# An encoder kernel: Lambda's exponential moved to the first down projection, no preparing transfers beside the output projection, another rounding order in the first two seven-product tiles

## The chip, the cores and the metric

The kernel runs on one core of a Trainium2 chip. A core has a matrix engine (TensorE, PE in the profile; its weight loads are shown as PEld), a vector engine (VectorE, DVE), a scalar engine (ScalarE, ACT), a general engine (GpSimd, POOL) and a sync engine (SyncE, SP), each with its own queue of instructions that it works off in order. SP, ACT and POOL can start transfers between device memory and on-chip memory. The metric is the device time of one execution in microseconds, taken as the median of several runs.

## The reference

A hybrid encoder of two layers on 512 positions of width 1024, float32:

```python
for l in range(DEPTH):
    h = rms_norm(x, norm_g[l, 0])
    x = x + 0.5 * swiglu(h, ffn_w_gate[l, 0], ffn_w_up[l, 0], ffn_w_down[l, 0])
    h = rms_norm(x, norm_g[l, 1])
    proj = h @ w_in[l]
...
    lam = jnp.exp(jnp.sum(lq[0] * lq[1])) - jnp.exp(jnp.sum(lq[2] * lq[3])) + lam_init
    yb = diff_attention(..., lam, lam_init, diff_subln_g[l], ...)
...
    x = x + merged @ w_o[l]
    h = rms_norm(x, norm_g[l, 2])
    x = x + 0.5 * swiglu(h, ffn_w_gate[l, 1], ffn_w_up[l, 1], ffn_w_down[l, 1])
return rms_norm(x, final_g)
```

`swiglu(h, g, u, d)` is `(silu(h @ g) * (h @ u)) @ d` with an inner width of 2816. Between the two halves of a layer stands the mixer: three attention branches (neighbourhood, differential, windowed with grouped keys), each gated, added up as `merged`, and projected by `w_o`. Lambda is one number per layer, an exponential of a sum minus another, used by the differential branch only.

## The kernel before

**Products.** Every float32 matrix product is made from operands split in two: a high part rounded by ACT (`scalar.copy` into the type fp32r) and a low part, the rest, made by DVE (`tensor_tensor` subtract). high x high, high x low and low x high are added up in PSUM. `weights` (L85) loads a weight tile of 512 KB through SP into one of three buffers `raw` and splits it (L92 on ACT, L93 on DVE); `parted` (L97) splits what is on the chip already (L100, L101).

**Order.** The program goes through ffn(0,0), mixer 0, ffn(0,1), ffn(1,0), mixer 1, ffn(1,1), the numbers being layer and half. A scheduler sorts the instructions of each engine by readiness and their place in the program. `tc.issue_after(x)` puts what is written in its block behind `x`, on the engine of `x` alone; `Seven.in_order` (L513) holds all instructions of its block in the written order on every engine.

**The seven-product tiles.** Each half has 22 tiles of 128 inner columns for gate and up. The first two (in ffn(0,0) four) are made as plain products and go through `gated` (L385): scale by the norm, Silu on ACT (L389), multiply (L390), split (ACT L124, DVE L126). The others go through `Seven.tile` (L593), which makes a tile's gate and up, each for two halves of the positions and of the channels, in seven block products where eight would be plain. Their moving sides are sums of blocks of the normed input, made once per half by `Sides` (L393, starting with L404 on DVE). Their weights are `wa` (the gate tile itself), `w31` and `w24` (two sums of weight blocks) and `w22`. A tile does, in this order: product 1 with `wa`; the copy of the former tile's bank (`sum22`, L688); the split of the next tile's `wa` (`next_wa`) and of its own `w24`; the former tile's Silu (L693); the copy of its own bank (L641); product 5 with `w31` (bank `pr`); product 4 of the former tile with `w22`; product 6 with `w24` (bank `mm`, moving side `pair`), which writes on into the bank that L641 has to read first; then products 2, 3 (bank `pv` and `pr`) and 7. Its scratch `gu` has two buffers, so the first such tile takes over the buffer of the first `gated`. In the first tile of a half, `next_wa` comes later (L661).

**Prepared sums.** In ffn(0,0) `w31` and `w24` are summed on the spot, by an accumulating transfer and by `others` on DVE (L551). For the three other halves they are prepared in device memory ahead of time by `prepare` (L447): each step copies a weight tile twice (ACT's queue, L474 and L475) and adds blocks onto copies of earlier tiles (three transfers on POOL's queue, L465). 27 steps make one half. `ahead_by` (L486) issues steps at a pace: each call of `weights` adds `owed[1]`, each seven-product tile adds `PACE["seven"]`, and a step is issued whenever a whole one is owed. `PACE` (L34) holds the rates by stage: a mixer calls `weights` 66 times before the output projection and 8 times in it; a down projection calls it 24 times. `drained` (L495) issues at the start of a half whatever of its steps is left.

**Small values.** `small_values` (L252) computes Lambda of both layers and some scaled constants, inside tile 8 of ffn(0,0), in written order, together with the first part of `position_tables` (L211); the rest of the position tables follows in tile 9. Silu and Exp need different tables on ACT; the change of table shows in the trace as ACT_TABLE_LOAD.

**Output projection.** The last loop of `mixer` (L1375) multiplies by `w_o` in eight tiles, adds to the residual (L1380, in tiles `lg` of the mixer's memory), stores the residual by POOL's queue (`x_keep`, L68) and makes the next norm's parts.

Of the kernel before, what the change touches and what calls it, by code (L numbers as in the profile page):

```python
# [11 lines left out]
F32 = mybir.dt.float32  # L12
# [4 lines left out]
P = 128  # L17
# [13 lines left out]
T5_STEPS = (8, 12, 16, 23, 32, 46, 64, 91)  # L31
GBUFS = 2 * MF
NO_WAIT = mybir.DependencyInfo(mybir.DependencyClass.NoSync, mybir.DependencyReason.DATA)
PACE = {"mixer": (0.42, 0.3), "seven": {(0, 1): 0.25}, "down": {(0, 0): 0.3, (0, 1): 0.4, (1, 0): 0.25}}  # L34
LOW_FIRST = (2, 4, 7)
WIDE, WIDE_FIRST = frozenset((2, 3, 4, 5, 6, 7)), frozenset((3, 4, 5))

# [2 lines left out]
def encoder(ctx: ExitStack, tc: tile.TileContext, a: dict, out: bass.AP):  # L40
# [13 lines left out]
    def f(ap):  # L54
        return ap.bitcast(F32)
# [23 lines left out]
    nc.scalar.activation(early, nhalf, AF.Silu)  # L79


    loaded, lower = [], []
    prepared, ahead, due, owed, queue = {}, [], [], [0.0, 0.0], {}

    def weights(src, width=1024):  # L85
# [163 lines left out]
            )  # L249
            own.append([bg, sg, sink, lq])  # L250

    def small_values(fp):  # L252
        for l in range(DEPTH):
            bg, sg, sink, lq = own[l]
            lam_init = 0.8 - 0.6 * math.exp(-0.3 * l)
            nc.vector.tensor_scalar_mul(bg, bg, 0.5)
            nc.vector.tensor_scalar_mul(sg, sg, 1.0 - lam_init)
            nsink = small.tile([P, 8], F32, tag=f"nsink{l}", name="nsink", bufs=1)
            nc.vector.tensor_scalar_mul(nsink, sink, -1.0)
            lp = fp.tile([P, 2, 64], F32, tag="g", name="lp", bufs=GBUFS)  # L260
            nc.vector.tensor_tensor(out=lp, in0=lq[:, :, 0, :], in1=lq[:, :, 1, :], op=ALU.mult)
            ls = small.tile([P, 2], F32, tag="ls", name="ls", bufs=1)
            nc.vector.reduce_sum(ls, lp, axis=mybir.AxisListType.X)
            nc.scalar.activation(ls, ls, AF.Exp)
            nlam = small.tile([P, 1], F32, tag=f"nlam{l}", name="nlam", bufs=1)
            nc.vector.tensor_tensor(out=nlam, in0=ls[:, 1:2], in1=ls[:, 0:1], op=ALU.subtract)
            nc.vector.tensor_scalar_add(nlam, nlam, -lam_init)
            own[l] = bg, sg, sink, nsink, nlam
# [12 lines left out]
    def ffn(l, i, h, nxt=None):  # L281

        with tc.tile_pool(name="ffn", bufs=1) as fp, ExitStack() as order:
# [11 lines left out]
            start, plain = (2, 4) if first else (0, 2)  # L295
            for m in range(start, MF):
                if m >= plain:
                    if first and m == plain + 4:
                        tables = position_tables(fp)
                        with tiles.in_order():  # L300
                            next(tables)
                            small_values(fp)
                    if first and m == plain + 5:
                        with tiles.in_order():
                            list(tables)
                    if m == plain:
# [52 lines left out]
            for m in range(KC):  # L359
                parts = []  # L360
                for c in range(0, MF, 8):
                    n = min(8, MF - c)
                    parts.append((c, n, cols(weights(a["w_down"][l, i, m, :, c * P : (c + n) * P]), n)))
                ps = mm_tile()
                for c, n, w in parts:
                    if m == 0 and c == 8:
                        tiles.flush()
                    for k in range(n):
                        nc.tensor.matmul(ps, w[k][0], ghi[c + k], start=c + k == 0, stop=False)  # L369
                        nc.tensor.matmul(ps, w[k][0], glo[c + k], start=False, stop=False)  # L370
                    for k in range(n):
                        nc.tensor.matmul(ps, w[k][1], ghi[c + k], start=False, stop=c + k == MF - 1)  # L372
                advance(m, ps, h.rb, fp, nxt)

    def quarters(fp):

        return fp.tile([P, 5, H], F32, tag="gu", name="gu", bufs=2)

    def keep(fp, un, ghi, glo):

        hi, lo = split(un, fp, "g", GBUFS)
        ghi.append(hi)
        glo.append(lo)

    def gated(h, fp, pg, pu, ghi, glo):  # L385
        t = quarters(fp).rearrange("p a c -> p (a c)")
        gn, un = t[:, 0:S], t[:, S : 2 * S]
        nc.vector.tensor_tensor(out=gn, in0=pg, in1=h.rb, op=ALU.mult)
        nc.scalar.activation(gn, gn, AF.Silu)  # L389
        nc.vector.tensor_tensor(out=un, in0=pu, in1=gn, op=ALU.mult)  # L390
        keep(fp, un, ghi, glo)

    class Sides:  # L393

# [107 lines left out]
    class Seven:  # L502


        def __init__(self, l, i, h, fp, sides, ghi, glo):
            self.at, self.h, self.fp, self.sides, self.out = (l, i), h, fp, sides, (ghi, glo)
            self.ready = (l, i) in prepared
            self.wide = WIDE if self.ready else WIDE_FIRST
            self.raw, self.even, self.sums, self.a22, self.wa, self.w31 = {}, {}, {}, {}, {}, {}
            self.tail, self.behind = (), {}  # L510

        @contextmanager
        def in_order(self):  # L513
# [79 lines left out]
        def tile(self, m):  # L593

            h, fp, sides, last = self.h, self.fp, self.sides, m == MF - 1
            first = not sides[0].t[3:]
            tail = iter(self.tail)

            def rest():
# [29 lines left out]
            with self.in_order():  # L629
# [1 line left out]
                self.fetch(m + 2)  # L631
                self.product(1, one, blocks(wa), [s.b11 for s in sides], start=True)
                rest()
                if not first:
                    next_wa()
                elif not self.ready:
                    self.others(m)
                parted(self.even.pop(m), w24)
                rest()
                u1 = self.halves(1)  # L640
                nc.scalar.copy(g[:, 0:u1], one[:, 0:u1])  # L641
# [60 lines left out]
                    add(q[3], one[:, 0], q[3])  # L702
                nc.vector.scalar_tensor_tensor(out=un, in0=un, scalar=-1.0, in1=gn, op0=ALU.mult, op1=ALU.mult)

            def kept():
                nc.scalar.copy(hi, un)
                nc.vector.tensor_tensor(out=lo, in0=un, in1=f(hi), op=ALU.subtract)

            self.tail = sum22, gate, fourth, up, kept

    def opening(l, i, h, fp, ghi, glo):

# [165 lines left out]
    def mixer(l, h, nxt):  # L878
        with tc.tile_pool(name="mix", bufs=1) as mp:
# [491 lines left out]
            while later:  # L1371
                step(None)
                run([last.pop(0)] if last else [])
            run([merge(2, m) for m in range(4)])
            for m in range(KC):  # L1375
                w = weights(a["w_o"][l, m])
                ps = mm_tile()
                product(ps, cols(w, KC), mh, ml)
                t = x_tile(m, l_tile())
                nc.vector.scalar_tensor_tensor(out=t, in0=ps, scalar=0.5, in1=t, op0=ALU.mult, op1=ALU.add)  # L1380
                x_keep(m, t, nxt.step)
                nxt.chunk(m, t, lambda: mp.tile([P, S], F32, tag="sq", name="sq", bufs=2))
# [8 lines left out]
    for l in range(DEPTH):  # L1391
# [2 lines left out]
        n2 = Norm(3 * l + 2, gain(l, 2))  # L1394
        owed[1] = PACE["mixer"][l]
        mixer(l, n1, n2)
        owed[1] = 0
        if l + 1 < DEPTH:
            h = Norm(3 * l + 3, gain(l + 1, 0))
            ffn(l, 1, n2, h)  # L1400
# [90 lines left out]
```

## Time and profile before

| | us |
|---|---|
| median of 3 runs | 2423.55 |
| lowest, highest | 2421.86, 2423.68 |
| the profiled execution | 2423.72 |
| its span, first to last instruction | 2421.9 |
| PE busy | 2393.2 (99%) |
| DVE busy | 1709.7 (71%) |
| ACT busy | 1330.8 (55%) |
| POOL busy | 361.1 (15%) |

Matmuls are pipelined and their ends are modelled, so a busy PE isn't PE at its peak. A row of the timeline holds the start, the length, the engine, the line of the kernel, the operation, what it writes and reads by the program's names, its shapes and the count of instructions merged into the row; a bracket at its end holds the idle time of the engine before it and what ended it. "issue" stands for time in which the engine waited for nothing that the profile shows. PEq, SPq and the like are the engines' queues.

### The profile page before, as it was taken

What the parts mean: (1) busy time and instruction counts of PE and PEld (TensorE: products, weight loads), DVE (VectorE), ACT (ScalarE), POOL (GpSimd) and SP (SyncE); (2) the same over time, 40 slices, a digit from 0 to 9 for tenths busy, and PEclk for the clock granted to TensorE, in tenths of its full rate; (3) what the DMA queues carried; (4) which work ended last, traced back from release to release, by engine and by line L of the source; (5) the groups of instructions that cost most, each with busy time, mean ns of one, the idle gap of its engine ahead of it and who ended that gap; (6) DMA issues with size and microseconds to landing.
All of it is one profiled execution on the core that took longest, in us unless ns stands there. A gap on an engine that the chain in (4) does not pass through costs nothing.

```text
span 2421.9 us, 34919 instructions
## 1 busy us (share of the span) xinstructions
PE 2393.2 (99%) x12762; PEld 2049.1 (85%) x12762; DVE 1709.7 (71%) x3061; ACT 1330.8 (55%) x2433; POOL 361.1 (15%) x524
## 2 busy tenths in 40 slices
PE   9999999999999999999999999999999999999998
PEld 7899888888888878888888888888888888888887
DVE  7999335766666669995389983467666666899832
ACT  6566225756566446663256652367565674566632
POOL 3100014432101120001200001144121100000000
PEclk9999999999999999999999999999999999999999
DMA  6576689986557697868745556788655624455532
GB/s 200 160 188 172 201 252 264 239 208 158 138 154 202 195 235 229 253 222 246 201 161 188 187 192 201 222 224 200 183 159 162 158 93 139 155 191 186 172 120 70
DMA packets 149771, 452.86 MB, mean 187 GB/s; under 512 B 18264, under 2 KB 23688, under 8 KB 148640
## 3 DMA queue, kind: packets, MB, share of 16 engines
q1 hardware_dynamic: 89856, 278.50, 34.8%
q0 software_dynamic: 40352, 107.36, 22.1%
q10 hardware_dynamic: 19392, 64.78, 7.5%
q8 instruction: 100, 1.64, 0.3%
q14 instruction: 71, 0.58, 0.1%
HBM read 428.52 MB, written 138.44 MB: 234 GB/s over the span
## 4 chain that ended last, share of the span: by engine, by line
PE 90%; DVE 4%; issue 2%; ACT 1%; DMA 1%; POOL 1%; SPq 0%; POOLq 0%; ACTq 0%; DVEq 0%
PE mm L562 17%; PE pr L562 8%; PE mm L117 8%; PE mm L115 8%; PE mm L114 8%; PE mm L369 5%; PE mm L372 5%; PE mm L370 5%; PE pv L562 4%; PE mm L1277 2%; PE av L1059 2%; PE mm L1273 2%; PE mm L1272 2%; PE t L1049 1%; PE s L1004 1%
## 5 line engine op out<-in xcount | busy, mean ns | idle before, releaser
L92 ACT CAST whi<-raw 128x1024 fp32r<-128x1024 f32 (+1 forms) x258 | 265.4, 1032 | 403.5 <-PE mm L370 185.4
L93 DVE TENSOR_TENSOR wlo<-raw,whi 128x1024 fp32r<-128x1024 f32 (+1 forms) x258 | 310.4, 1203 | 233.3 <-ACT whi L92 118.6
L114 PE MATMUL mm<-h,whi 128*128 128x512 f32 x800 | 318.2, 398 | 0.0
L115 PE MATMUL mm<-h,whi 128*128 128x512 f32 x800 | 314.1, 393 | 0.0
L369 PE MATMUL mm<-g,whi 128*128 128x512 f32 x528 | 205.4, 389 | 0.0
L370 PE MATMUL mm<-g,whi 128*128 128x512 f32 x528 | 205.4, 389 | 0.0
L117 PE MATMUL mm<-h,wlo 128*128 128x512 f32 x800 | 197.9, 389 | 0.0
L101 DVE TENSOR_TENSOR wlo<-raw,whi 128x1024 fp32r<-128x1024 f32 x156 | 184.2, 1218 | 5.5 <-ACT whi L100 5.5
L117 PEld LDWEIGHTS mm<-h,wlo 128*128 128x128 f32 x800 | 150.0, 188 | 31.3
L115 PEld LDWEIGHTS mm<-h,whi 128*128 128x128 f32 x800 | 150.5, 188 | 29.1 <-DVE h L146 0.3
L114 PEld LDWEIGHTS mm<-h,whi 128*128 128x128 f32 x800 | 150.4, 188 | 28.8 <-ACT h L145 0.3
L100 ACT CAST whi<-raw 128x1024 fp32r<-128x1024 f32 x156 | 156.9, 1052 | 16.4 <-DMA raw<-in_w_gu 13.9
L372 PE MATMUL mm<-g,wlo 128*128 128x512 f32 x528 | 131.4, 389 | 0.0
L1018 ACT ACTIVATE lg<-lg,negm 128x256 f32<-128x256 f32 (+1 forms) x192 | 114.1, 594 | 25.4 <-DVE negm L1015 24.2
L370 PEld LDWEIGHTS mm<-g,whi 128*128 128x128 f32 x528 | 99.1, 188 | 20.6
L372 PEld LDWEIGHTS mm<-g,wlo 128*128 128x128 f32 x528 | 99.1, 188 | 20.6
L369 PEld LDWEIGHTS mm<-g,whi 128*128 128x128 f32 x528 | 99.1, 188 | 20.6
L688 ACT COPY gu<-mm 128x512 f32<-128x512 f32 (+1 forms) x78 | 41.9, 538 | 126.1 <-PE mm L562 124.4
L614 DVE TENSOR_TENSOR gu<-pr,gu 128x256 f32<-128x256 f32 x234 | 98.2, 420 | 5.3 <-ACT gu L647 2.7
L465 POOL DMA_DIRECT2D d_odd<-in_w_gu x60 | 52.1, 868 | 294.9 <-DMA d_odd<-in_w_gu 237.7
L100 ACT CAST whi<-wsum 128x1024 fp32r<-128x1024 f32 x78 | 82.1, 1053 | 24.2 <-PE pv L562 24.2
L101 DVE TENSOR_TENSOR wlo<-wsum,whi 128x1024 fp32r<-128x1024 f32 x78 | 94.8, 1215 | 0.0
(312 smaller groups left out, 5797.4 us busy)
## 6 DMA issues: line engine op xcount, KB each, us to landing
raw<-in_w_gu SPq DMA_DIRECT2D x94, 512.0 KB, 3.4
d_odd<-in_w_gu ACTq DMA_DIRECT2D x60, 512.0 KB, 5.2
d_even<-in_w_gu ACTq DMA_DIRECT2D x60, 512.0 KB, 6.2
d_odd<-in_w_gu POOLq DMA_DIRECT2D x60, 512.0 KB, 7.8
wsum<-d_odd SPq DMA_DIRECT2D x60, 512.0 KB, 3.3
raw<-d_even SPq DMA_DIRECT2D x60, 512.0 KB, 4.4
raw<-in_w_down SPq DMA_DIRECT2D x48, 512.0 KB, 4.2
raw<-in_w_gate SPq DMA_DIRECT2D x48, 512.0 KB, 4.8
```

Of the source, the lines that this page charges most:

```text
L92: nc.scalar.copy(hi[:, w], raw[:, w])
L93: lower[:] = [nc.vector.tensor_tensor(out=lo[:, w], in0=raw[:, w], in1=f(hi[:, w]), op=ALU.subtract).ins]
L100: nc.scalar.copy(hi, src)
L101: nc.vector.tensor_tensor(out=lo, in0=src, in1=f(hi), op=ALU.subtract)
L114: nc.tensor.matmul(ps, wh, xhi[k], start=k == 0, stop=False)
L115: nc.tensor.matmul(ps, wh, xlo[k], start=False, stop=False)
L117: nc.tensor.matmul(ps, wl, xhi[k], start=False, stop=k == n - 1)
L369: nc.tensor.matmul(ps, w[k][0], ghi[c + k], start=c + k == 0, stop=False)
L370: nc.tensor.matmul(ps, w[k][0], glo[c + k], start=False, stop=False)
L372: nc.tensor.matmul(ps, w[k][1], ghi[c + k], start=False, stop=c + k == MF - 1)
L562: nc.tensor.matmul(out, wk, bk, start=go, stop=end, skip_group_check=True)
L1018: nc.scalar.activation(p, p, AF.Exp, bias=negm, scale=-1.0, accum_out=total)
```

## The change

Lambda's two sums per layer (`lambda_sums`, DVE alone) are made in tiles 7 and 8 of ffn(0,0), one layer in each; the position tables move to tiles 9 and 10; the exponential and the constants move behind tile 1 of the first down projection, without a written order. The pace in the mixers goes from 0.42 and 0.30 to 0.48 and 0.31 steps per weight tile and is 0 beside the output projection; in ffn(0,1) it goes from 0.25 to 0.29 per seven-product tile and from 0.40 to 0.43 in the down projection. In the first seven-product tile of a prepared half, DVE's low part of `w24` goes behind the low part of the first `gated` tile; in the second tile of every half, the split of the next `wa` goes behind that of `w24`.

```diff
-PACE = {"mixer": (0.42, 0.3), "seven": {(0, 1): 0.25}, "down": {(0, 0): 0.3, (0, 1): 0.4, (1, 0): 0.25}}
+PACE = {"mixer": (0.48, 0.31), "seven": {(0, 1): 0.29}, "down": {(0, 0): 0.3, (0, 1): 0.43, (1, 0): 0.25}}
...
-    def small_values(fp):
+    def lambda_sums(fp, l):
+        lq = own[l][3]
+        lp = fp.tile([P, 2, 64], F32, tag="g", name="lp", bufs=GBUFS)
+        nc.vector.tensor_tensor(out=lp, in0=lq[:, :, 0, :], in1=lq[:, :, 1, :], op=ALU.mult)
+        ls = small.tile([P, 2], F32, tag=f"ls{l}", name="ls", bufs=1)
+        nc.vector.reduce_sum(ls, lp, axis=mybir.AxisListType.X)
+        own[l][3] = ls
+
+    def small_values():
         for l in range(DEPTH):
...
-            lp = fp.tile([P, 2, 64], F32, tag="g", name="lp", bufs=GBUFS)
-            nc.vector.tensor_tensor(out=lp, in0=lq[:, :, 0, :], in1=lq[:, :, 1, :], op=ALU.mult)
-            ls = small.tile([P, 2], F32, tag="ls", name="ls", bufs=1)
-            nc.vector.reduce_sum(ls, lp, axis=mybir.AxisListType.X)
             nc.scalar.activation(ls, ls, AF.Exp)
...
-                    if first and m == plain + 4:
+                    if first and m in (plain + 3, plain + 4):
+                        with tiles.in_order():
+                            lambda_sums(fp, m - plain - 3)
+                    if first and m == plain + 5:
                         tables = position_tables(fp)
                         with tiles.in_order():
                             next(tables)
-                            small_values(fp)
-                    if first and m == plain + 5:
+                    if first and m == plain + 6:
                         with tiles.in_order():
                             list(tables)
...
                 advance(m, ps, h.rb, fp, nxt)
+                if first and m == 1:
+                    small_values()
...
-        keep(fp, un, ghi, glo)
+        hi, lo = [fp.tile([P, S], F32R, tag="g", name="g", bufs=GBUFS) for _ in range(2)]
+        nc.scalar.copy(hi, un)
+        kept.append(nc.vector.tensor_tensor(out=lo, in0=un, in1=f(hi), op=ALU.subtract).ins)
+        ghi.append(hi)
+        glo.append(lo)
...
             first = not sides[0].t[3:]
+            second, self.turned = not first and not self.turned, not first
...
-                if not first:
+                if first and not self.ready:
+                    self.others(m)
+                if not (first or second):
                     next_wa()
-                elif not self.ready:
-                    self.others(m)
-                parted(self.even.pop(m), w24)
+                with ExitStack() as order:
+                    if first and self.ready:
+                        order.enter_context(tc.issue_after(kept[-2]))
+                    parted(self.even.pop(m), w24)
+                if second:
+                    next_wa()
...
             run([merge(2, m) for m in range(4)])
+            owed[1] = 0
             for m in range(KC):
                 w = weights(a["w_o"][l, m])
...
         mixer(l, n1, n2)
-        owed[1] = 0
```

More of the change, by code (lines that the diff above doesn't have):

```diff
@@ L79, in encoder @@
     nc.scalar.activation(early, nhalf, AF.Silu)
-    loaded, lower = [], []
+    loaded, lower, kept = [], [], []
     prepared, ahead, due, owed, queue = {}, [], [], [0.0, 0.0], {}
@@ L250, in small_loads @@
             own.append([bg, sg, sink, lq])
-    def small_values(fp):
+    def lambda_sums(fp, l):
[6 more added lines that the diff above has]
+    def small_values():
         for l in range(DEPTH):
-            bg, sg, sink, lq = own[l]
+            bg, sg, sink, ls = own[l]
             lam_init = 0.8 - 0.6 * math.exp(-0.3 * l)
@@ L373, in ffn @@
                 advance(m, ps, h.rb, fp, nxt)
+                if first and m == 1:
+                    small_values()
     def quarters(fp):
         return fp.tile([P, 5, H], F32, tag="gu", name="gu", bufs=2)
[L379 to L383, printed above, removed]
     def gated(h, fp, pg, pu, ghi, glo):
@@ L509, in __init__ @@
             self.raw, self.even, self.sums, self.a22, self.wa, self.w31 = {}, {}, {}, {}, {}, {}
-            self.tail, self.behind = (), {}
+            self.tail, self.behind, self.turned = (), {}, False
         @contextmanager
@@ L703, in up, with keep @@
                 nc.vector.scalar_tensor_tensor(out=un, in0=un, scalar=-1.0, in1=gn, op0=ALU.mult, op1=ALU.mult)
-            def kept():
+            def keep():
                 nc.scalar.copy(hi, un)
                 nc.vector.tensor_tensor(out=lo, in0=un, in1=f(hi), op=ALU.subtract)
-            self.tail = sum22, gate, fourth, up, kept
+            self.tail = sum22, gate, fourth, up, keep
     def opening(l, i, h, fp, ghi, glo):
```

## The prediction

> **What bounds the kernel now.** Three of the changed parts aim at stalls of PE, so the list of PE's waits is read first: columns are what PE waited for, total us, times, longest.
>
> ```profile
> PE mm L562 <- ACT gu L641: 6.0, 8, 2.8
> PE mm L562 <- DVE wlo L101: 3.1, 4, 0.9
> PE mm L562 <- ACT gu L688: 1.9, 1, 1.9
> ...
> PE pr L562 <- ACT whi L100: 1.3, 1, 1.3
> ```
>
> PE is the bound nearly everywhere, and the waits that are left sit in the seven-product tiles (L562). The timeline then says which tiles. First the ones around Lambda's exponential, in ffn(0,0); a tile's length is the distance between two starts of product 5 (`pr<-pair,whi`).
>
> ```profile
> 84.02 1.09 PE L562 MATMUL pr<-pair,whi 128*128 128x512 f32 x4
> ...
> 84.76 2.35 DVE L101 TENSOR_TENSOR wlo<-raw,whi 128x1024 fp32r<-128x1024 f32 x2
> ...
> 87.77 0.64 PE L562 MATMUL mm<-pair,wlo 128*128 128x256 f32 x4
> ...
> 91.07 1.28 ACT L264 ACT_TABLE_LOAD   x1
> ...
> 93.96 1.09 PE L562 MATMUL pr<-pair,whi 128*128 128x512 f32 x4
> ...
> 94.81 0.29 DVE L261 TENSOR_TENSOR lp<-lq 128x128 f32<-128x128 f32 x1
> ...
> 95.13 0.28 DVE L263 TENSOR_REDUCE ls<-lp 128x2 f32<-128x128 f32 x1
> 95.45 0.20 ACT L264 ACTIVATE ls<-ls 128x2 f32<-128x2 f32 x1 [3.10 <-DVE ls L263]
> ...
> 97.38 0.91 PE L562 MATMUL mm<-h,w22l 128*128 128x256 f32 x4 [1.86 <-ACT gu L688]
> ...
> 99.24 1.28 ACT L693 ACT_TABLE_LOAD   x1
> ...
> 101.48 2.08 PE L562 MATMUL mm<-pair,whi 128*128 128x256 f32 x8 [1.48 <-ACT gu L641]
> ...
> 108.74 0.65 PE L220 MATMUL st<-hot,parts 64*36 64x512 f32 x2
> ...
> 110.30 0.68 DVE L222 TENSOR_SCALAR td<-st 36x512 f32<-36x512 f32 x1
> ...
> 110.85 1.09 PE L562 MATMUL pr<-pair,whi 128*128 128x512 f32 x4
> ...
> 111.84 0.17 DVE L228 MEMSET td<- 8x128 f32 x1
> ```
>
> A tile takes 93.96 - 84.02 = 9.94 us; the one with the exponential takes 110.85 - 93.96 = 16.89. ACT loads its table, stands 3.10 us for DVE's sums, does two tiny exponentials, and only then makes the copy (L688) that PE needs; the table for Silu comes back in front of the next copy (L641). The windows add the clock (columns: length; busy us and count of PE, PEld, DVE, ACT, POOL; granted clock; DMA share; GB/s):
>
> ```profile
> 81.31:91.25 9.94, 9.94 (x74) 9.41 (x74) 9.61 (x16) 6.47 (x13) 0.86 (x1) 1.00 0.73 197
> 91.25:108.24 16.99, 13.65 (x81) 12.19 (x81) 12.95 (x33) 8.85 (x15) 0.86 (x1) 0.80 0.46 128
> ```
>
> A mean of 0.80 over 16.99 us is 6.8 us at half clock. And DVE, busy 9.61 of 9.94 us, has only 0.33 us to spare per tile here.
>
> Next the entry of ffn(0,1), against that of ffn(1,1), which has no preparing transfers before it:
>
> ```profile
> 871.85 0.76 POOL L68 DMA_DIRECT2D d_x<-lg  x1
> ...
> 880.51 1.29 DVE L404 TENSOR_TENSOR xf<-h 128x512 f32<-128x512 f32 x2 [7.24 <-issue]
> ...
> 887.70 0.65 PE L185 MATMUL st<-ident,rs 128*128 128x128 f32 x4 [0.28 <-POOL rs L178]
> ...
> 896.60 1.17 PE L562 MATMUL pr<-pair,whi 128*128 128x512 f32 x4 [1.29 <-ACT whi L100]
> ...
> 898.18 0.74 PE L562 MATMUL pr<-pair,wlo 128*128 128x256 f32 x4 [0.41 <-DVE wlo L101]
> ...
> 901.75 1.19 PE L562 MATMUL mm<-pair,whi 128*128 128x512 f32 x4 [2.83 <-ACT gu L641]
> ...
> 2073.11 1.29 DVE L404 TENSOR_TENSOR xf<-h 128x512 f32<-128x512 f32 x2 [0.60 <-DMA d_x<-lg]
> ```
>
> The sides (L404 on) live in memory that the mixer's last stored residual still occupies. In ffn(0,1) that store is issued at 871.85 behind preparing transfers on the same POOL queue, and DVE stands 7.24 us; in ffn(1,1) it stands 0.60. DVE is then late through the whole first tile, and PE waits four times.
>
> Last, the first three tiles of ffn(1,0), standing for the other prepared halves:
>
> ```profile
> 1242.17 1.21 DVE L101 TENSOR_TENSOR wlo<-raw,whi 128x1024 fp32r<-128x1024 f32 x1
> ...
> 1243.30 1.28 DVE L126 TENSOR_TENSOR g<-gu,g 128x512 fp32r<-128x512 f32 x2
> ...
> 1244.07 0.37 ACT L641 COPY gu<-mm 128x256 f32<-128x256 f32 x1 [1.17 <-DVE g L126]
> ...
> 1244.50 1.19 PE L562 MATMUL mm<-pair,whi 128*128 128x512 f32 x4 [0.53 <-ACT gu L641]
> ...
> 1254.50 2.35 DVE L101 TENSOR_TENSOR wlo<-raw,whi 128x1024 fp32r<-128x1024 f32 x2
> ...
> 1256.91 0.75 PE L562 MATMUL mm<-pair,wlo 128*128 128x256 f32 x4 [0.95 <-DVE wlo L101]
> ...
> 1263.94 2.35 DVE L101 TENSOR_TENSOR wlo<-raw,whi 128x1024 fp32r<-128x1024 f32 x2
> ...
> 1266.82 0.64 PE L562 MATMUL mm<-pair,wlo 128*128 128x256 f32 x4
> ```
>
> In the first tile the copy L641 needs the buffer that the first L126 frees, and L126 stands behind the rounding of w24 (L101). In the second tile w24's low part is the second of two L101, and PE needs it first. Each wait shifts PE by about 0.2 us more than its idle time shows, since matmul ends are modelled.
>
> **The change, part by part.**
>
> *Exponential.* The stalled tile loses 16.89 - 9.94 = 6.95 us, less 0.58 for the two matmuls of L220, which stay: **6.4 us go**. What comes back is DVE work, put in four tiles instead of one. A sum is 0.6 us (94.81 to 95.41). In tile 7 DVE is done at 87.11 for a matmul at 87.77: 0.6 us of room, so the first sums just fit. Tile 8 gives 0.33 and takes 0.6: a wait of about 0.3. Tile 9 takes two tiny casts. Tile 10 gets the position tables, 1.7 us of DVE (110.30 to 112.01) against 0.58 by which L220 holds PE, the 0.33 and little room: a wait of about 0.6. With 0.1 to 0.2 per restart and a little more because PE comes earlier, 1.4 us. Net **-5.0**; between -3.4 (twice the waits) and -6.4 (DVE takes it all up). The exponentials and one table load, 1.28 + 2 x 0.20 us of ACT, go into the first down projection, where ACT stands waiting for PE before its weight casts; the page's row:
>
> ```profile
> L92 ACT CAST whi<-raw 128x1024 fp32r<-128x1024 f32 (+1 forms) x258 | 265.4, 1032 | 403.5 <-PE mm L370 185.4
> ```
>
> So they cost nothing; without that cover, 1.7 us. Nothing in between needs Silu, so the mixer's first load should go too: five loads instead of seven. [...]
>
> *Transfers.* Counting the steps: before, 7 in the down projection, 27 in the mixer ahead of w_o, 4 beside w_o; after, 7, 31 and 0, so all 27 of ffn(0,1) are issued either way and none bunches at its start. ffn(0,1) then starts like ffn(1,1): four waits of 0.28 + 1.29 + 0.41 + 2.83 = 4.8 us go, and 0.2 to 0.25 each with them: **-5.8**. What is late next is the second tile, as everywhere. At least 0, if something else holds the entry; at most 6. The seven-product stage of ffn(0,1) gets six steps instead of five, the first right in its opening tiles, where DVE has no room: **+0.4** (0 to 1.5). The last two steps that ffn(1,0) now issues at its start come earlier: 0.
>
> The four moved steps go past POOL's and SP's queues in the mixer, whose opening is tight:
>
> ```profile
> 379.45 0.88 POOL L465 DMA_DIRECT2D d_odd<-in_w_gu  x1 [1.27 <-issue]
> ...
> 391.47 0.81 POOL L465 DMA_DIRECT2D d_odd<-in_w_gu  x1 [6.40 <-issue]
> ...
> 396.82 2.54 POOL L1088 TENSOR_TENSOR nab<-mask,rp 128x256 f32<-128x256 f32 x3
> ```
>
> A step holds POOL for 12.0 us there (379.45 to 391.47), and the bias of the second head (L1088) waits behind three of them; behind the bias, SP's next loads. By the count, the steps that stood at weights 5, 7 and 10 of the mixer now stand at 4, 6 and 8: as many ahead of that bias, each earlier. I take **0**, with -1.2 (bias earlier) to +12 (one step more ahead of it).
>
> *Order.* In the first tile only DVE's half of w24 goes behind the first L126. In ffn(1,0) L126 can then start near 1242.3, L641 near 1243.1, and PE's 0.53 us goes: **-0.8** with its restart. Its price, w24's low part 1.3 us later, fits: it is needed 0.9 us after product 6 starts. In the second tile the swap brings that part 1.2 us earlier and the wait of 0.95 goes. But it comes back: DVE runs without a break through the third tile, done at 1266.29 for a matmul at 1266.82. PE, 1.2 us earlier, finds 0.5 us of room and waits for the rest. So the gain is that room less a restart, 0.37 us in each prepared half, three of them, and in ffn(0,0) by the same reading of its tiles about 0.25: **-1.35**. Bounds: 0, and -4.2 if all four waits (3.1 us in the list, with their restarts) go for good.
>
> The sum is -5.0 - 5.8 + 0.4 - 0.8 - 1.35 = **-12.5 us**. The profiled execution took 2423.72 us, 2421.9 of it span, 0.17 above the median of the three runs: 2411.2.
>
> **The rivals.**
>
> *The order pays whole* (0.12): DVE does not pass the lateness on to the third tile. For it: the second roundings, which now come last, are needed only a tile later. Against: no gap in DVE from 1254.5 to 1266.3. 2.9 us more: 2408.3.
>
> *The entry of ffn(0,1) stays late* (0.07): the stored residual waits for bandwidth anyway. Against it: 0.60 us in ffn(1,1). 5.8 less: 2417.0.
>
> *The half clock stays* (0.05). At half clock for 6.8 us, 1.5 of them idle, PE lost 2.7 us; if not the stall brought it, this stays, or falls on another stall: 2413.9. For it: the 2.83 us wait at 901.75 is longer than the 1.86 before this drop, and the rows behind it run at full speed. Against: it starts with the stall. [...]
>
> *The mixer's opening is bound by POOL* (0.16). If one step more than now stands ahead of the second head's bias, the softmax of that head and the loads behind it come 12.0 us later with nothing to hide it: 2423.2, no change (0.11). From two on it decides for the other side: 24 - 12.5 = +11.5, 2435.2, slower (0.05). For it: waits of PE just after already hang on this chain. Against: the count above.
>
> **How the numbers follow.** My forecast, 2411.2, gets 0.60. A measurement of this kernel tells about 0.2%, 4.85 us, from no change: below 2418.7 is faster. Forecast and the first three rivals are faster: 0.84; one step on POOL is the same: 0.11; two are slower: 0.05. The range leaves out POOL's cases and takes the bounds of the others, 2406.5 (order whole, DVE taking up the sums) to 2418.5 (entry late, some waits doubled).
>
> **What would show it.** Right: no table load among the seven-product tiles and five in all; clock 1.00 from 90 to 110; tile lengths there of 9.9 to 10.9; DVE's L404 of ffn(0,1) within 1 us of its last sum and no wait in its first tile; the first-tile wait of ffn(1,0) gone; the 0.95 of the second tile replaced by about 0.6 in the third. Wrong: bias L1088 of the second head later than 397 with PE idle behind it, or the first tile of ffn(0,1) still longer than 8.5 us.

## The result, and the profile after

The changed kernel takes **2445.3 us** (median of 5 runs, 2444.38 to 2448.4) where the kernel before takes 2423.55 (five runs beside it): a ratio of 1.0094, 95% interval 1.0079 to 1.0108, so 22 us **slower**. The forecast was 2411.2. The tiles of the four feed-forward halves became 7.6 us shorter in the profiled execution; some 29 us were lost elsewhere. PE's waits after, in the same columns as those of before:

```profile
PE t L1061 <- ACT lg L1138: 5.7, 1, 5.7
PE mm L568 <- ACT gu L653: 5.1, 9, 1.9
PE st L176 <- DVE acc L157: 3.4, 1, 3.4
PE t L1061 <- POOL lg L1128: 1.9, 1, 1.9
PE t L1156 <- DVE tot L1214: 1.8, 1, 1.8
```

The second row is what is left in the seven-product tiles (L568). The other four belong to the two mixers (L1061, L1156) and to the opening (L176) and add up to 12.8 us. Two of the four are new; the first and the last stood in the list before with 1.0 and 0.9 us. But waits are not all of it. Cut both timelines of PE at the first and the last product 5 (`pr<-pair,whi`) of each half; the cuts of the first half, before:

```profile
53.69 0.40 PE L562 MATMUL pr<-pair,whi 128*128 128x512 f32 x1
...
230.23 0.40 PE L562 MATMUL pr<-pair,whi 128*128 128x512 f32 x1
```

and after, with the next three cuts:

```profile
59.36 0.40 PE L568 MATMUL pr<-pair,whi 128*128 128x512 f32 x1
...
230.45 0.40 PE L568 MATMUL pr<-pair,whi 128*128 128x512 f32 x1
...
907.58 0.40 PE L568 MATMUL pr<-pair,whi 128*128 128x512 f32 x1
...
1097.78 0.40 PE L568 MATMUL pr<-pair,whi 128*128 128x512 f32 x1
...
1255.67 0.40 PE L568 MATMUL pr<-pair,whi 128*128 128x512 f32 x1
```

Between such cuts, in us of the one profiled execution of each kernel (the last row ends with PE's last matmul; the last four columns are experiments, told below; p_old's start has a first load of weights in it that landed late, a wait of 2.8 us, and best1's execution is the fastest of its runs). The mixer rows differ between executions: a_pad40 and a_pad40_dve have the same instructions in the mixers, and these rows lie 2.6 and 3.7 us apart.

| stage | before | after | a_pad40 | a_pad40_dve | p_old | best1 |
|---|---|---|---|---|---|---|
| start to first product 5 | 53.69 | 59.36 | 60.43 | 54.62 | 57.61 | 53.89 |
| tiles of ffn(0,0) | 176.54 | 171.09 | 171.71 | 171.73 | 171.02 | 171.58 |
| down (0,0), mixer 0, entry of ffn(0,1) | 666.37 | 677.13 | 669.28 | 671.88 | 668.32 | 664.36 |
| tiles of ffn(0,1) | 191.41 | 190.20 | 186.91 | 186.72 | 190.30 | 186.54 |
| down (0,1), entry of ffn(1,0) | 154.39 | 157.89 | 154.38 | 154.39 | 154.38 | 154.38 |
| tiles of ffn(1,0) | 187.54 | 186.69 | 186.37 | 186.36 | 186.36 | 186.36 |
| down (1,0), mixer 1, entry of ffn(1,1) | 663.92 | 670.10 | 664.62 | 668.35 | 661.41 | 661.27 |
| tiles of ffn(1,1) | 186.73 | 186.66 | 186.38 | 186.38 | 186.36 | 186.38 |
| last tile and last projection | 133.67 | 136.71 | 133.67 | 133.67 | 133.64 | 133.64 |

The tiles of ffn(0,0) are 5.45 us shorter and those of ffn(1,0) 0.85, as hoped. The row to stop at is the fifth: down (0,1) has no wait of PE in either kernel and no line of the change in its loop, and yet takes 3.50 us more. So does the last projection, 3.04. The groups of the page say how. Before (columns: count, busy us, mean ns of one):

```profile
L369 PE MATMUL mm<-g,whi 128*128 128x512 f32 x528 | 205.4, 389 | 0.0
L370 PE MATMUL mm<-g,whi 128*128 128x512 f32 x528 | 205.4, 389 | 0.0
L117 PE MATMUL mm<-h,wlo 128*128 128x512 f32 x800 | 197.9, 389 | 0.0
L372 PE MATMUL mm<-g,wlo 128*128 128x512 f32 x528 | 131.4, 389 | 0.0
```

and after, the same four:

```profile
L376 PE MATMUL mm<-g,whi 128*128 128x512 f32 x528 | 209.3, 396 | 0.0
L375 PE MATMUL mm<-g,whi 128*128 128x512 f32 x528 | 207.8, 394 | 0.0
L117 PE MATMUL mm<-h,wlo 128*128 128x512 f32 x800 | 198.4, 390 | 0.0
L378 PE MATMUL mm<-g,wlo 128*128 128x512 f32 x528 | 134.9, 395 | 0.0
```

Every matmul that reads `g` is 5 to 7 ns longer; the one that reads `h` is not. From start to start, in PE's records, it is 226.7 ns before and 233.3 after: 6.6 ns for 1584 matmuls are 10.5 us. The matmuls that read the mixer's merged and branch tiles (`mh`, `ml`, `yp`) and those of the last projection show the same and add 7.3, so that about **17.8 us** stand in rows that wait for nothing.

What these operands share is where they are allocated. The change gives the sums of Lambda a tag for each layer (`ls0`, `ls1`) where there was one `ls`, which makes one more slot of 32 bytes in the pool `small`; the pools `ffn` and `mix` lie behind it and start at byte 90560 of a partition in place of 90528. `h` and the weight tiles lie ahead of it and stay. Before the change all of them begin 160 bytes above a multiple of 256 (`h` at 1952, the weights at 34720, `g` at 90528).

**The opening** is 5.67 us longer. DVE before, then DVE after:

```profile
19.72 3.87 DVE L157 TENSOR_TENSOR acc<-acc,sq 128x512 f32<-128x512 f32 x5
```

```profile
19.51 0.17 DVE L264 TENSOR_SCALAR bg<-bg 128x24 f32<-128x24 f32 x1
20.09 0.15 DVE L265 TENSOR_SCALAR sg<-sg 128x1 f32<-128x1 f32 x1 [0.41 <-DMA sg<-in_subln_g]
22.43 0.17 DVE L267 TENSOR_SCALAR nsink<-sink 128x8 f32<-128x8 f32 x1 [2.19 <-DMA sink<-in_gqa_sink]
22.52 0.69 DVE L157 TENSOR_TENSOR acc<-acc,sq 128x512 f32<-128x512 f32 x1
25.08 0.18 DVE L264 TENSOR_SCALAR bg<-bg 128x24 f32<-128x24 f32 x1 [1.88 <-DMA bg<-in_b_gate]
```

These are the scalings of `small_values`, written in the first down projection and run at the start of the kernel. The call lost its `with tiles.in_order()`, which had tied it to its place, and without it the scheduler takes whatever has its inputs first. On DVE they stand ahead of the norm's sums and wait for small loads that land late; the sums end late, and PE stands 3.44 us for them at 31.27.

**The exponentials** didn't go where they are written either. ACT, after:

```profile
91.31 1.28 ACT L268 ACT_TABLE_LOAD   x1
92.61 0.20 ACT L268 ACTIVATE ls<-ls 128x2 f32<-128x2 f32 x1
...
100.47 1.28 ACT L705 ACT_TABLE_LOAD   x1
...
103.75 1.28 ACT L268 ACT_TABLE_LOAD   x1
105.04 0.20 ACT L268 ACTIVATE ls<-ls 128x2 f32<-128x2 f32 x1
...
111.14 1.28 ACT L705 ACT_TABLE_LOAD   x1 [0.22 <-DVE gu L690]
```

They stay in the seven-product tiles, one in each of two tiles, and the kernel has nine table loads, not five. The stall of before is gone all the same: the sums come in earlier tiles, so that ACT finds them ready.

**Mixer 0** pays in its opening. Before, the second load of a gate weight is waited for by ACT like this:

```profile
408.00 1.05 ACT L92 CAST whi<-raw 128x1024 fp32r<-128x1024 f32 x1 [2.72 <-DMA raw<-in_w_gate]
```

After, in the timelines of POOL, SP, ACT and PE:

```profile
401.10 2.52 POOL L1100 TENSOR_TENSOR nab<-mask,rp 128x256 f32<-128x256 f32 x3
403.30 0.47 POOL L1128 MEMSET lg<- 128x128 f32 x1
403.45 1.09 POOL L471 DMA_DIRECT2D d_odd<-in_w_gu  x1
...
404.64 0.34 SPq L91 DMA_DIRECT2D raw<-in_w_gate  x1
...
415.28 1.05 ACT L92 CAST whi<-raw 128x1024 fp32r<-128x1024 f32 x1 [6.80 <-DMA raw<-in_w_gate]
...
422.03 0.45 PE L1061 MATMUL t<-ident,lg 128*128 128x128 f32 x1 [5.73 <-ACT lg L1138]
```

A preparing step starts 1.2 us ahead of that load; the cast comes 10.6 us after the load's issue, and PE stands 5.73 us. From about 418.4 to 425.3, in the stall and behind it, the clock is down as well (columns: length; busy us and count of PE, PEld, DVE, ACT, POOL; granted clock; DMA share; GB/s):

```profile
416.00:436.00 20.00, 14.27 (x72) 12.28 (x71) 15.22 (x34) 15.46 (x40) 7.67 (x16) 0.83 0.82 234
```

### The profile page after: what moved, and what is told of

Its sections match the earlier page's. It is cut to its first block, busy times and chain, and to the rows that moved or that the text cites. A ratio compares the mean times of both kernels' runs of the same rounds, so it can differ in the third digit from the quotient of the medians.

```text
span 2443.5 us, 34897 instructions
## 1 busy us (share of the span) xinstructions
PE 2410.9 (99%) x12762; PEld 2048.4 (84%) x12762; DVE 1708.5 (70%) x3061; ACT 1333.5 (55%) x2435; POOL 361.0 (15%) x524
## 4 chain that ended last, share of the span: by engine, by line
PE 90%; DVE 4%; issue 2%; ACT 2%; DMA 1%; POOL 1%; POOLq 0%; DVEq 0%; ACTq 0%
PE mm L568 16%; PE mm L117 8%; PE mm L115 8%; PE mm L114 8%; PE pr L568 8%; PE mm L376 5%; PE mm L378 5%; PE mm L375 5%; PE pv L568 4%; PE mm L1289 2%; PE av L1071 2%; PE mm L1285 2%; PE mm L1284 2%; PE t L1061 1%; DVE wlo L101 1%
## 5 line engine op out<-in xcount | busy, mean ns | idle before, releaser
L376 PE MATMUL mm<-g,whi 128*128 128x512 f32 x528 | 209.3, 396 | 0.0
L375 PE MATMUL mm<-g,whi 128*128 128x512 f32 x528 | 207.8, 394 | 0.0
```

## The experiments

Each theory here has its rival: the slower matmuls could come from the transfers that run beside them, the opening from its own late loads, the mixer's gaps from chance. The first set takes the changed kernel apart; the kernel before took 2425.1 us beside it (median of 29 runs).

**a_pad40 and b_pad56: the memory.** The pool `small` holds a tile that is only padding. Cut by 32 bytes in the changed kernel, enlarged by 32 in the kernel before:

```diff
-    small.tile([P, 48], F32, tag="pad", name="pad", bufs=1)
+    small.tile([P, 40], F32, tag="pad", name="pad", bufs=1)
```

This is a_pad40; b_pad56 has 56 in the same place.

> The changed kernel with its padding tile in the pool small cut from 48 to 40 words, so that every tile of the pools ffn and mix lies again where it lay before the change (32 bytes lower); nothing else differs. Theory of the memory shift: the matmuls that read 512 columns from these pools go back from 234 to 227 ns each, which is 10.5 us in the down projections, 3.0 in the last projection, 2.3 in the output projections and 2.0 in the merges of the branches: 17.8 us less than the changed kernel, 2427.5 us, and the groups of the down projection and of the last projection at 389 ns again. Rival, the slower matmuls come from the preparing transfers running beside them: nothing changes, 2445.3 us and 396 ns.

> The kernel before with its padding tile enlarged from 48 to 56 words, so that the pools ffn and mix lie 32 bytes higher, where the change puts them; nothing else differs. Theory of the memory shift: 17.8 us more than before, 2441.3 us, with 396 ns in the down and last projections. Rival (the transfers, or the changed order): 2423.6 us and 389 ns.

Measured: 2428.75 us (ratio to before 1.0018, 1.0007 to 1.0030) and 2440.89 (1.0068, 1.0051 to 1.0085). Taken out of the change, the move gives back 16.6 us by the medians (the two were measured beside different runs of the kernel before; by the two ratios it is 18); put alone into the kernel before, it costs 15.8. One row of each, a_pad40 and then b_pad56:

```profile
L376 PE MATMUL mm<-g,whi 128*128 128x512 f32 x528 | 205.4, 389 | 0.0
```

```profile
L370 PE MATMUL mm<-g,whi 128*128 128x512 f32 x528 | 209.3, 396 | 0.0
```

The transfers run the same in both kernels of each pair, so that rival falls. Three quarters of the loss is a tile of 8 bytes.

**a_pad40_dve and a_pad40_both: where the small values run.** The call is tied to its place again, first on DVE, then on ACT too:

```diff
                 if first and m == 1:
-                    small_values()
+                    with tc.issue_after(lower[0]), tc.issue_after(nxt.squared):
+                        small_values()
```

(`lower[0]` is DVE's last rounding of weights, `nxt.squared` ACT's last square; a_pad40_dve has the first of the two alone.)

> As the run before last (changed kernel, padding tile of 40 words), and DVE's part of the small values (the six scalings and the two subtractions) is ordered behind the last rounding of weights of the first down projection's second output tile, so that it can't be scheduled into the opening. Theory: the scalings stood ahead of the norm's sums, behind small loads that land late, and cost 5.7 us in the opening (first product 5 of ffn(0,0) back from 59.4 to 53.7 us): 2421.8 us. Rival, the opening was late because its own weights landed late: 2427.5 us, first product 5 near 59.

> As the run before, and ACT's part of the small values (the two exponentials) is also ordered, behind the square of the first down projection's second output tile: the exponentials then really run in that projection, and the four table loads among the seven-product tiles of ffn(0,0) go. Theory: their cost in those tiles is what tiles 3 to 6 take above 9.9 us less the sums and the position tables, about 1 us: 2420.8 us, two table loads fewer than in the kernel before and four fewer than in the changed one. Rival, the exponentials in the down projection hold up PE there: 2422 us or more.

Measured: 2423.14 us (0.9994, 0.9984 to 1.0004) and 2422.07 (0.9991, 0.9979 to 1.0004). The scalings cost 5.6 us, and the table shows them where they were looked for: the opening is 54.62 us where a_pad40 has 60.43. DVE's sums in a_pad40_dve stand as before:

```profile
19.27 3.87 DVE L157 TENSOR_TENSOR acc<-acc,sq 128x512 f32<-128x512 f32 x5
```

The exponentials in the tiles cost 1.1 us by the medians, the size expected but less than these two can tell apart; the tiles of ffn(0,0) in the profile say 0.7 (171.73 to 171.03; the rest of a_pad40_both's profiled execution, its slowest run, is left out of the table). The time alone would also fit the rival, 2422 or more; the trace does not, since PE has no wait around the two exponentials in the down projection. With both tied there are five table loads, the count that the prediction gave.

**p_old and best1: the transfers.** p_old puts the old rates back, and the old end of the transfers, behind the output projection; only the exponential and the order of the roundings are left of the change. best1 takes from the change that no transfers run beside the output projection, and puts their four steps into the first down projection:

```diff
-PACE = {"mixer": (0.48, 0.31), "seven": {(0, 1): 0.29}, "down": {(0, 0): 0.3, (0, 1): 0.43, (1, 0): 0.25}}
+PACE = {"mixer": (0.42, 0.3), "seven": {(0, 1): 0.25}, "down": {(0, 0): 0.467, (0, 1): 0.46, (1, 0): 0.285}}
...
             run([merge(2, m) for m in range(4)])
-            owed[1] = 0
+            owed[:] = [0.0, 0.0]
```

> The changed kernel with the padding tile of 40 words and the small values ordered into the first down projection on both engines (the last run of the first set), and with the old rates of the preparing transfers and the old place where they end (beside the output projection they run again): what is left of the change is the exponential and the order of the roundings. Theory: the new rates cost about 6.1 us from the end of ffn(0,0) to ffn(0,1) and 3.3 us in the second mixer (means of the three profiles) and save 4.2 us inside ffn(0,1), so that undoing them gives 2422.1 - 5.2 = 2416.9 us; the first tile of ffn(0,1) takes about 12.3 us again and the gap of PE ahead of the first transposes of the mixer (5.7 to 7.2 us) goes. Rival, that gap belongs to something else (the loads of the mixer landing late by chance): 2422 + 5.8 = 2427.9 us.

> As the run before, but no preparing transfers beside the output projection, as the change wants it: the four steps go into the first down projection (rate 0.467 in place of 0.3, eleven steps for seven), and the mixers keep the old rates and the old weights at which their steps fall (2, 5, 7, 10, 12 and on); the later rates are set so that the second mixer's steps fall where they fell before the change. Theory: this takes the gain at the entry of ffn(0,1) without the loss in the mixers: 2416.9 - 4.2 - 1.5 = 2411.2 us, first tile of ffn(0,1) 8.43 us, no gap of PE over 2 us in the mixers. Rival, the first down projection or the mixer has no room for the four steps: a gap appears there and the time stays at 2417 or above.

Measured: 2417.56 us (0.9970, 0.9960 to 0.9980) and **2414.0** (0.9951, 0.9938 to 0.9965), beside 2425.23 of the kernel before. So the new rates, taken as a whole, cost 4.5 us; with the steps moved elsewhere, the same wish gains 3.6 over p_old by the medians, though the two intervals overlap. Part of the 4.5 us may lie in the second mixer (664.62 and 668.35 with the new rates, 661.27 to 663.92 with the old), which no run takes apart. best1 is the fastest kernel here, some 11 us ahead of the kernel before. Its interval doesn't tell 2414.0 from the 2411.2 expected.

**best1_early: one thing put back.** In best1's first mixer alone, the first 15 weights get the changed kernel's rate:

```diff
-        ahead_by(owed[1])
+        ahead_by(0.48 if fast[0] > 0 else owed[1])
+        fast[0] -= 1
...
+        fast[0] = 15 if l == 0 else 0
         mixer(l, n1, n2)
```

> The best version so far (2414.0 us; padding tile of 40 words, small values ordered, four steps of the transfers moved from the output projection to the first down projection, old mixer rates), with one thing of the change put back: in the first mixer the first 15 weights have the rate 0.48, so that the steps fall at weights 2, 4, 6, 8, 11, 13 and 15 as in the changed kernel in place of 2, 5, 7, 10, 12 and 14. Theory: the early steps bring the step that runs beside the second head's gate weight and with it the gap of PE of 5 to 7 us near 415 us and the half clock behind it, some 7.5 us: 2421.5 us. Rival, the loss in the mixer comes from the rate of its later part (0.48 to its end): no gap over 2.5 us near 415 and 2414 us.

Measured: 2418.6 us (0.9979, 0.9969 to 0.9988): 5.0 us faster than before in place of best1's 11.2, so 6.2 us go with the place of a few steps. The gap is back. PE in best1, then in best1_early:

```profile
409.83 0.41 PE L1062 MATMUL t<-ident,lg 128*128 128x128 f32 x2 [1.24 <-ACT lg L1139]
```

```profile
412.14 0.57 PE L1019 MATMUL s<-qk 128*128 128x256 f32 x1 [4.21 <-DVE negm L1030]
```

Laid side by side, the timelines of SP, POOL, ACT and PE show two ways to the gap. Times are us behind the last product 5 of ffn(0,0); "step ahead" is the last preparing step on POOL that starts before the gate load is issued:

| kernel | step ahead | gate load issued | ACT casts it | ACT waited | largest gap of PE near it |
|---|---|---|---|---|---|
| before | 161.2 | 170.2 | 177.8 | 2.7 | under 0.7 |
| p_old | 161.4 | 170.5 | 178.5 | 3.9 | under 0.7 |
| best1 | 161.6 | 170.8 | 179.8 | 4.9 | 1.2 |
| a_pad40 | 169.7 | 170.8 | 182.5 | 7.9 | 6.5 |
| a_pad40_dve | 170.0 | 171.2 | 182.8 | 8.2 | 7.2 |
| a_pad40_both | 169.6 | 170.8 | 184.0 | 9.5 | 6.1 |
| best1_early | 166.5 | 174.6 | 183.0 | 6.3 | 4.2 |

In the first way, the three a_pad40 kernels, a step begins about 1 us ahead of the gate load, and the cast comes 11.7 to 13.2 us after the load's issue (10.6 in the changed kernel itself). In the first three rows it is 7.6 to 9.0. In the six kernels whose names begin with b_, which have the old rates as well, it is 7.3 to 10.3; their largest gaps of PE there are 0.4 to 1.5 us, and 2.6 in b_pad56, the one with 10.3. So a late load also comes by chance, but only the early steps bring gaps of 4 us and more. That the step slows the load is read from this and not shown by an experiment of its own.

best1_early goes the other way: its load is not slower (8.5 us) but issued nearly 4 us later. POOL and SP in best1, then in best1_early:

```profile
392.03 0.82 POOL L472 DMA_DIRECT2D d_even<-d_even  x1 [1.38 <-issue]
392.58 2.70 POOL L1101 TENSOR_TENSOR nab<-mask,rp 128x256 f32<-128x256 f32 x3
...
396.30 0.33 SPq L91 DMA_DIRECT2D raw<-in_w_gate  x1
```

```profile
395.25 0.82 POOL L474 DMA_DIRECT2D d_even<-d_even  x1 [0.74 <-issue]
395.80 2.52 POOL L1103 TENSOR_TENSOR nab<-mask,rp 128x256 f32<-128x256 f32 x3
...
399.34 0.33 SPq L92 DMA_DIRECT2D raw<-in_w_gate  x1
```

The bias of the second head stands behind the last transfer of a step on POOL, and the gate load goes out behind the bias. With the step 4.9 us later behind the cut, the bias comes 3.9 us later and the load with it. Either way ACT stands at this cast (7.9 to 9.5 us in the three a_pad40 kernels, 6.3 in best1_early) with the softmax behind it in its queue, and PE waits for the softmax.

**b_pad64, b_const32, b_gap32, b_pad128, b_pad256: what about the memory counts.** All are the kernel before with more padding: `[P, 64]`, `[P, 80]` and `[P, 112]` in place of `[P, 48]` (64, 128, 256 bytes), or 32 bytes ahead of all pools (b_const32, the first two lines below), or 32 bytes between the pool of `h` and that of the weights (b_gap32, the last three):

```diff
-    early = const.tile([P, 8], F32, tag="early", name="early")
+    early = const.tile([P, 16], F32, tag="early", name="early")
...
+    gap = ctx.enter_context(tc.tile_pool(name="gap", bufs=1))
+    gap.tile([P, 8], F32, tag="gap", name="gap", bufs=1)
     wpool = ctx.enter_context(tc.tile_pool(name="wpool", bufs=4))
```

> The kernel before with its padding tile enlarged from 48 to 64 words: the pools ffn and mix lie 64 bytes higher than before the change, at the same place within 64 bytes (32). Theory, what counts is the place within 64 bytes: 2423.6 us, 389 ns in the down projection. Rival, any move from the old place costs: near 2440 us, 396 ns.

> The kernel before with a constant tile ahead of every pool enlarged by 32 bytes, so that everything behind it moves by 32 bytes: the normalized inputs h, the weights, and the pools ffn and mix alike, all at 0 within 64 bytes where they were at 32. Theory, the place of the moving operand alone counts: the matmuls on h slow down as well, some 2400 of 512 columns by 7 ns, about 16 us on top of 16: about 2456 us. Rival, only the place of the moving operand against that of the weights counts: 2423.6 us.

> The kernel before with a tile of 32 bytes put between the pool of the normalized inputs h and that of the weights: h stays, the weights and the pools ffn and mix move together by 32 bytes. Theory, the place of the moving operand against that of the weights counts: the down and last projections keep 227 ns (389 ns in the groups), and the 2472 matmuls of 512 columns on h take 234: about 16.6 us more, 2441 us. Rival, the place against h or against the fixed tiles counts, or the place itself: the down projection goes to 396 ns and h stays at 227.

> The kernel before with the pools ffn and mix 128 bytes higher. A look at the time between matmuls of the down projection: 227 ns if the place counts within 128 bytes, 229 to 234 if within a longer stretch.

> The kernel before with the pools ffn and mix 256 bytes higher. A look at the time between matmuls of the down projection: 227 ns if the place counts within 256 bytes, 229 to 234 if within a longer stretch or not by a period.

| kernel | `g` against the weights | ns from start to start, on `g` | on `h` (`mm<-h,wlo`) | time, us |
|---|---|---|---|---|
| before | 0 | 227 | 227 | 2423.6 to 2425.2 |
| b_pad56 | +32 | 234 | 227 | 2440.9 |
| b_pad64 | +64 | 229 | 227 | 2429.3 |
| b_pad128 | +128 | 232 | 227 | 2438.2 (one run) |
| b_pad256 | +256 | 227 | 227 | 2421.4 (one run) |
| b_const32 | 0, all moved | 227 | 227 | 2424.2 |
| b_gap32 | 0, `h` left behind | 227 | 233 | 2439.4 |

The first idea, the place within 64 bytes, fell twice: at +64 it is not 227, and in b_const32, with every operand where the slow ones were, nothing is slow. The rival of the second run won, and b_gap32 turns it round: there the weights and `g` move together and stay fast, `h` is left behind and slows down. Two rows of b_gap32:

```profile
L119 PE MATMUL mm<-h,wlo 128*128 128x512 f32 x800 | 203.0, 395 | 0.0
...
L374 PE MATMUL mm<-g,wlo 128*128 128x512 f32 x528 | 131.4, 389 | 0.0
```

So what counts for these matmuls is the distance between the moving operand and the tiles of the weights' side, and 256 bytes on it is as good as 0. That the partner is the weight tile itself is the likeliest reading, since PE reads both; the tiles that move with the weights in all these kernels (the raw weights, the working tiles) were not separated from it. Nor is the distance all: in the seven-product tiles of the kernel before, at the same distance, the matmuls of 512 columns on `h` take 227 ns in `pr<-h,whi` and 233 in `pv<-h,whi` (medians), and b_pad64, which moves neither operand, brings the second to 227. What makes that difference stays open.

Not tried: the order of the roundings alone. At 2 us it is below what a comparison can tell, and the tiles show it.

## Why the prediction was wrong, and where it was right

*Exponential*: **wrong in its place, right in its size.** The step that failed is "the exponentials and one table load [...] go into the first down projection, where ACT stands waiting for PE [...] So they cost nothing". It took the place in the program text for the place in the queue. They stayed in the tiles (0.7 to 1.1 us), and the same call's DVE scalings, which the prediction didn't price at all, went into the opening (5.6 us). Once tied, ACT's part does cost nothing and there are five loads. The size had some luck in it: the half clock that the prediction read in the stalled tile is not there in every execution. In b_const32 and b_pad128, which keep the old exponential, the same tile has full clock and takes 15.5 us in place of 16.89.

*An unpriced term*: no step of the prediction asked what the second `ls` does to memory. It was the largest term, 16.6 us, and an argument from waits, queues and engine time can't find it: the diff shows a new tag, and only the addresses show the rest.

*Transfers*: the entry of ffn(0,1) came as said. DVE's first sums there, after:

```profile
886.76 1.29 DVE L410 TENSOR_TENSOR xf<-h 128x512 f32<-128x512 f32 x2 [0.54 <-DMA d_x<-lg]
```

They wait 0.54 us for the stored residual where they waited 7.24, and the first tile takes 8.43 us where it took 12.28. The step that failed is the mixer's opening: "By the count [...] I take **0**". The count of steps ahead of the second head's bias was right, eight before and after. The sign that the prediction named came all the same: the bias starts at 401.10, later than 397, with PE idle behind it. But that lateness is not the steps' doing. Behind the cut the bias starts at 170.7 us, and at 170.2 in b_pad56, which has the old rates and the memory of the change; before, it is 166.6. In a_pad40, with the memory put back, it is 167.3, and the gap is there too. What the prediction left out is the other neighbour: a step just ahead of a load that ACT waits for. The rival *mixer's opening is bound by POOL* had the stage and the sign, and its chain (step, bias, load) is the one in best1_early, with as many steps ahead of the bias as in best1, only later. Its price was too high: 12.0 us is the distance between the starts of two steps and not the time that one holds POOL, and best1_early shows 3.9 us at the bias and 6.2 in the whole time. The added step in ffn(0,1), +0.4, was about right: the tiles there take 186.91 and 186.72 us in a_pad40 and a_pad40_dve, 186.54 in best1, which lacks the step. The 190.20 of the changed kernel has a wait of 1.88 us that neither of the two shows. Both transfer terms together: -5.4 foretold, +4.5 measured.

*Order*: right, in the two halves where nothing hides it. The first tile of ffn(1,0) takes 8.43 us in place of 9.23 (-0.80 foretold and found); its second and third together 20.93 in place of 21.29, so 0.36, foretold 0.37; in ffn(1,1) it is 0.38. In ffn(0,1) a wait of 1.41 us in the third tile hides it. The wait does come back in the third tile, and the rival *order pays whole* falls.

Exponential and order together, as the prediction priced them: -7.15. p_old has these two alone, tied: 7.7 us less than before (4.8 to 9.7 by its interval). The steps from there to the changed kernel, -7.7 + 4.5 + 5.6 + 1.1 + 16.6 = +20.1, are differences from one kernel to the next, so that their sum closes by itself, up to the 1.7 us by which the medians of the kernel before differ. What stands apart from that sum is b_pad56, where the memory alone costs 15.8.

Two bounds of the prediction don't come out of its own terms: twice the waits leave -3.6 of the exponential's 6.4, not -3.4, and the lower end of the range is 2406.9 by the two terms that it names, not 2406.5. Neither matters beside an error of 34 us.

*The half clock*: that rival fell for the tiles. After the change the window from 90 to 110 us has full clock, though three table loads lie in it. It moved to new stalls: at those of 3.44 us (PE goes on at 31.27), 5.73 (422.03) and 1.84 (523.61) the records show half clock for 3.4, 6.8 and 3.4 us, from about 1.5 us behind the first, 3.6 us before the end of the second and 0.7 us behind the third. The last stall is as short as the one of 1.86 before, which has 6.8 us of half clock from about 0.4 us behind it. The length of a stall does not settle whether the clock falls: the 2.83 us of the first tile of ffn(0,1) have no half clock behind them in the profile of before and 3.4 us of it in b_pad64 and b_pad256, where the same stall is as long to 0.01 us.

## What to carry to other kernels

A call moved in the program text is moved in the queues only if something ties it there: look for the ordering context that the old place had, and price what the scheduler will do with every instruction of the call, not only the one that the change is about. When a new tile, tag or buffer is added, compare the addresses of what lies behind it, and if matmuls without waits get longer by a few ns, move the pool back before looking for anything else. And a background transfer is placed by the load that follows it: count not only what it holds up on its own queue but which awaited load is in flight beside it, and what has to be done before that load can be issued.

## What the runs showed of the hardware

In the long rows of matmuls of 512 fp32r columns of the down projections, the time of one went with where its moving operand lies against the tiles of the weights' side. From start to start it was 227 ns at a distance of 0 (before, b_const32) or 256 bytes (b_pad256), 234 at 32 (b_pad56), 229 at 64 (b_pad64) and 232 at 128 (b_pad128), the distance counted within 256 bytes; on `h`, with the weights moved 32 bytes away from it, 233 (b_gap32). In this kernel 32 bytes in one pool are 16 us (15.8 in b_pad56, 16.6 in a_pad40), 0.7% of the time, without any wait in the rows that grow. Whether the partner is the weight tile itself these runs do not separate.

Half clock came in stretches of 3.4 or 6.8 us at stalls of PE: 6.8 at one of 1.86 us before, 3.4, 6.8 and 3.4 at those of 3.44, 5.73 and 1.84 us after. The stall of 2.83 us in the first tile of ffn(0,1) brought 3.4 us of it in b_pad64 and b_pad256 and none in the profile of before.
